# A relative-position bias table in DRAM: one copy and reversed queries in place of 128 shifted copies

## The chip, the cores and the metric

The kernel runs on one core of a Trainium2 chip. The metric is the device time of one launch in microseconds (us). A core has a matrix engine (TensorE, PE in the profile), a vector engine (VectorE, DVE), a scalar engine (ScalarE, ACT), GpSimd (POOL) and SyncE (SP), which here only issues DMAs. Each engine works through its own queue of instructions strictly in order. 16 DMA engines move the data.

## The reference

A trunk of two layers on 256 tokens of 1024 channels, all float32. Layer 0 has a feed-forward block, differential attention, a second feed-forward block and a gated embedding; layer 1 has a state-space mixer in place of the attention. What matters here is the bias of the attention scores: it depends only on the distance between query and key, through a table of 32 buckets and 16 columns (8 heads with two softmax maps each).

```
def diff_attention(h, w_qkv, w_o, lam_vecs, subln_g, rel_bias, lambda_init):
    ...
    def block(args):
        q_blk, blk = args
        q_pos = blk * Q_BLOCK + jnp.arange(Q_BLOCK, dtype=jnp.int32)
        dist = q_pos[:, None] - k_pos[None, :]
        bias = rel_bias.astype(jnp.float32)[t5_bucket(dist)]
        bias = bias.reshape(Q_BLOCK, S, N_HEADS, 2).transpose(2, 3, 0, 1)
        s = jnp.einsum('bhmqd,bhmkd->bhmqk', q_blk, k).astype(jnp.float32) + bias
        s = jnp.where(dist >= 0, s, NEG_INF)
        prob = jax.nn.softmax(s, axis=-1)
        attn = prob[:, :, 0] - lam * prob[:, :, 1]
        return jnp.einsum('bhqk,bhkv->bhqv', attn.astype(v.dtype), v)
    ...
    o = rmsnorm(o, subln_g) * (1.0 - lambda_init)
    o = o.transpose(0, 2, 1, 3).reshape(Bsz, S, D_MODEL)
    return o @ w_o
```

## The kernel before

The 256 tokens are two blocks of 128 (b = 0 and 1), each with its own x tile. Weights come as tiles of [128, 1024] float32 (512 KB, `raw`): SP issues one DMA for each, ScalarE casts it to float32r (`hi`, line 131), VectorE subtracts to get the rest (`lo`, line 133). There are three `raw` buffers, so the fourth load waits until the `lo` of the first has been computed. Both blocks use a weight tile, and every product is three matmuls: hi by hi (line 302), lo by hi (303), hi by lo (304).

The first feed-forward block works in column groups c. A group of block b has two PSUM banks (`up`), one for the gate and one for the linear part. When both are summed, ScalarE takes `sg`, the SiLU of the gate bank (line 444), VectorE multiplies it with the other bank (`h`, line 446), and TensorE transposes `h` (`hT_ps`, line 449). There are four banks in all, which the group c = 0 of both blocks fills. The first matmul of group c = 1 therefore waits for the first `sg`. Eight weight tiles make up a group.

At the start the program also prepares what the attention wants later, in low priority and so mixed into the first feed-forward block. The bias is one of these. GpSimd fills `tab` [16, 384] in 32 copies (line 535): one row for each softmax map, with the bias of distance d at index 255 - d and a large negative number from index 256 on, for keys that come after the query. Then `tab` goes to DRAM as `tab_d` [128, 16, 384], one copy per query, by eight DMAs of SP of 16 copies each (line 539): 128 x 16 x 384 x 4 bytes = 3.1 MB. In the attention a head's bias is one DMA (line 581) of 128 rows, one per query. Its partition step in DRAM is one element less than a copy, so each row starts one element earlier in its own copy. The bias tiles have three buffers; the first three loads depend on `tab_d` alone and are issued in the first feed-forward block, the other 13 in the attention. `tab` comes from the pool `work` with the tag "sg", which has two buffers and serves the `sg` tiles of the feed-forward too: the second `sg` waits until the DMAs have read `tab`.

The queries go to `qz` by a VectorE copy from PSUM (line 675, eight times), and the normalised outputs of four heads are transposed and split into `oT` by one ScalarE and one VectorE instruction (lines 321 and 322 from line 642, four times).

The order on each engine is made by a scheduler from priorities and its own estimates of time, so a change in one place can move instructions elsewhere.

Of the kernel before, what the change touches and what calls it, by code (L numbers as in the profile page):

```python
# [9 lines left out]
F32 = mybir.dt.float32  # L10
# [6 lines left out]
P = 128  # L17
# [5 lines left out]
# Places in the schedule, by layer (f01: block 0, second ffn) or by norm (block, norm, token half).  # L23
# [49 lines left out]
def bucket_ranges(n_buckets=32, max_dist=128, n=256):  # L73
    """[start, stop) of the distances in each causal T5 bucket."""
    exact = n_buckets // 2
    of = []
    for d in range(n):
        if d < exact:
            of.append(d)
        else:  # L80
            large = exact + int(math.log(d / exact) / math.log(max_dist / exact) * (n_buckets - exact))
            of.append(min(large, n_buckets - 1))
    return [(of.index(b), n - of[::-1].index(b)) for b in range(n_buckets)]


class Weights:
    """Streams weight tiles [128, 1024] from DRAM and splits each into two float32r parts, or takes two tiles unsplit."""
# [35 lines left out]
    def flush(self, force):  # L123
        """Splits what is loaded, up to the limit."""
        nc = self.nc
        while self.pending and self.pending[0][0] < max(self.split_limit, force + 1):
            n, raw = self.pending.pop(0)
            hi = self.split_pool.tile([P, 1024], F32R, tag="hi", name=f"hi{n}")
            lo = self.split_pool.tile([P, 1024], F32R, tag="lo", name=f"lo{n}")
            with self.hold[0]():  # L130
                nc.scalar.copy(hi, raw)  # L131
            with self.hold[1]():
                (nc.gpsimd if n in self.on_pool else nc.vector).tensor_tensor(lo, raw, hi.bitcast(F32), ALU.subtract)  # L133
            self.tiles[n] = (hi, lo)
# [8 lines left out]
def trunk(ctx, tc, x, p, norm_g, ffn_w_in, ffn_w_out, attn_w_qkv, attn_w_o, attn_lam, attn_subln_g,  # L143
          rel_bias, ssm_lam_re, ssm_lam_im, ssm_log_dt, ssm_b_re, ssm_b_im, ssm_c_re, ssm_c_im, ssm_d, ssm_w_glu,
          ssm_b_glu, ple_w_proj, ple_w_gate, out):
    nc = tc.nc
# [8 lines left out]
    dram = ctx.enter_context(tc.tile_pool(name="dram", bufs=1, space=bass.MemoryType.DRAM))  # L155
# [5 lines left out]
    def extra_banks(name):  # L161
        """The last two banks serve one section after another."""
        if "cm" in ps_extra:
            ps_extra["cm"].__exit__(None, None, None)
        ps_extra["cm"] = tc.tile_pool(name=name, bufs=1, space=bass.MemoryType.PSUM)
        ps_extra["pool"] = ps_extra["cm"].__enter__()
# [126 lines left out]
    def after_transposes(b, key, left):  # L293
        """The second block's last products of a layer leave room for the first block's transposes of the next."""
        at, step = OPT["at"].get(key, (0, 1))
        n = (at - left) // step + 1 if at else 0
        if b == 0 or n <= 0 or not marks.get(0):
            return nullcontext()
        return tc.issue_after(marks[0][min(2 * n, KT) - 1])
# [62 lines left out]
    def post_norm(b, halves, gain, factor, name):  # L362
        """x += factor * rmsnorm(m) with m in two [128, 512] PSUM banks."""
        xb = xs[b]
        parts = []
# [26 lines left out]
    def two_halves(b, accs, hi, lo, units, key):  # L392
        """Products over k into both halves; the last units finish the first half before the second."""
        tail = OPT["tail"].get(key, 1)
        for k in range(len(units)):
            take(b, units[k])
            ks = [k] if k < len(units) - tail else range(len(units) - tail, len(units)) if k == len(units) - 1 else []
            for j in range(2):
                sl = slice(j * 512, (j + 1) * 512)
                for kk in ks:  # L400
                    wh, wl = W.tiles[units[kk]]
                    left = (len(units) - k) * 2 if len(ks) == 1 else 2 * len(ks)
                    left -= j * len(ks) + kk - ks[0]
                    with after_transposes(b, key, left):
                        mm3(accs[j], hi[:, kk, :], lo[:, kk, :], wh[:, sl], wl[:, sl], kk == 0, kk == len(units) - 1)
            yield

# [108 lines left out]
    if any(st[0] == "attn" for st in stages):  # L516
# [7 lines left out]
        # bias of every softmax map by j = key - query + 127 (distance 255 - j), masked beyond 255  # L524
# [11 lines left out]
        # one copy per query: a stride of one less than a copy then shifts the table by the query  # L536
        tab_d = dram.tile([P, 16, 384], F32, name="tab_d")
        for j in range(8):
            nc.sync.dma_start(tab_d[16 * j:16 * j + 16].rearrange("r m j -> m r j"),
                              tab.rearrange("m (o j) -> m o j", o=1).broadcast_to([16, 16, 384]))  # L540
# [34 lines left out]
    def scores(b, h):  # L575
        kT = shared["kT"]
        nk = P * (b + 1)
        nm = f"{h}_{b}"
        bias = attn_pool.tile([P, 2, 256], F32, tag="bias", name=f"bias{nm}", bufs=3)
        src = tab_d[0, 2 * h:2 * h + 2, 127 + 256 - nk:127 + 256 - nk + 1]  # L580
        nc.sync.dma_start(bias[:, :, 0:nk], bass.AP(tensor=src.tensor, offset=src.offset,
                                                      ap=[[16 * 384 - 1, P], [384, 2], [1, nk]]))
# [34 lines left out]
    def attention(b, qkv_units, pj_units, o_units):  # L617
# [9 lines left out]
        def normed(grp, on):  # L627
# [11 lines left out]
            for h in range(4):  # L639
                nc.tensor.transpose(pt[:, h * P:(h + 1) * P], on[:, h, :], ident)  # L640
            split_T(pt, oT_hi[:, grp * 4:grp * 4 + 4, :].rearrange("p a t -> p (a t)"),
                    oT_lo[:, grp * 4:grp * 4 + 4, :].rearrange("p a t -> p (a t)"), sub_g)
# [8 lines left out]
        for n, (part, grp) in enumerate(QKV_ORDER):  # L651
# [21 lines left out]
            if part == 0:  # L673
                for m in range(2):
                    (nc.vector.tensor_copy if m >= OPT["qz"] else nc.scalar.copy)(
                        qz[b][64 * m:64 * m + 64, :, m, :], ptv[64 * m:64 * m + 64])
# [41 lines left out]
    def exact_exp(out_, in_, n, nm):  # L718
        """exp to float32 accuracy: 2^(m / 16) times a short series of the rest."""
# [14 lines left out]
    def ssm_exp():  # L734
        """lambda, lambda * dt and the moduli |a|^k with states (e, p) on partitions, columns (q, g'): group 16q + 2g' + e."""
# [20 lines left out]
    def ssm_tables(pool, keep):  # L756
# [7 lines left out]
        # sine and cosine of lambda_im * dt: reduced to [-pi, pi], polynomials of the half angle  # L764
# [24 lines left out]
        # powers of a = rho e^(i theta), then of the phase and of the modulus by squaring  # L789
# [16 lines left out]
        # phases of a^(8j), moduli of a^8  # L806
# [23 lines left out]
        # (a - 1) / lambda  # L830
# [23 lines left out]
        # the norm's gain of the input channels goes into b and d  # L854
# [11 lines left out]
        # output matrices with states on partitions  # L866
# [82 lines left out]
        # skip connection on the diagonal, Toeplitz rows to DRAM behind seven zero blocks  # L949
# [20 lines left out]
    def ssm_u(b):  # L970
        """x and the norm's factors to the layout (channel group, block) x (step, channel) through DRAM."""
# [35 lines left out]
    def ssm_core(pool, vs, tos):  # L1007
# [35 lines left out]
        def grouped(out_ap, st_, w, **flags):  # L1043
            """One product per channel group: 32 stationary columns and 128 moving columns each."""
# [288 lines left out]
```

## Time and profile before

| | |
|---|---|
| device time, median of 3 runs | 1148.12 us (1147.39 to 1149.25) |
| span of the profiled execution | 1145.0 us |
| TensorE busy | 1049.3 us (92%) |
| VectorE busy | 694.8 us (61%) |
| ScalarE busy | 554.4 us (48%) |
| GpSimd busy | 241.3 us (21%) |
| moved by DMA | 221.74 MB, mean 194 GB/s |

The span runs from the first to the last instruction of the one profiled execution. Its own device time is not listed beside it; the median of the timed runs lies 3.1 us above the span, which is what lies around it. Times inside the trace count from the span's start. "Waited for" always names what ended a wait.

### The profile page before, as it was taken

The page shows a single profiled execution, that of the slowest core. Times are in us where ns is not written, and L with a number is a line of the kernel's source. Part 1 is how long each engine was busy: PE and PEld are TensorE (multiplying, and loading weights), DVE is VectorE, ACT ScalarE, POOL GpSimd, SP SyncE. Part 2 cuts the span into 40 slices and gives each one's busy share as a digit, 9 for nine tenths or more (in the row PEclk, how much of TensorE's full clock was granted, in tenths as well). Part 3 has the DMA queues.
Part 4 walks back from the last instruction along what each step waited for, and adds up shares of the span by engine and source line. Part 5 has one row for each costly group of instructions (what it writes and reads, how often), then busy time and mean ns, then how long its engine had stood idle before and what let it go on. Part 6 is the DMA issues. An engine that isn't in the chain of part 4 may idle for free.

```text
span 1145.0 us, 14323 instructions
## 1 busy us (share of the span) xinstructions
PE 1049.3 (92%) x5123; PEld 839.2 (73%) x5123; DVE 694.8 (61%) x1011; ACT 554.4 (48%) x873; POOL 241.3 (21%) x289
## 2 busy tenths in 40 slices
PE   6599999999998999999787997999966999999997
PEld 4478888878776787777665776888744878888885
DVE  5166554659838897555678563655358576555464
ACT  5255444556765544443455542544343465444454
POOL 6000000000012004888889400000122010000001
PEclk9799999999999999999998998999987999999999
DMA  8976655646439667666556579756693557564651
GB/s 219 163 246 210 186 189 192 200 145 211 157 128 207 181 192 203 202 206 223 176 165 198 142 204 308 236 200 208 207 358 137 172 178 220 184 186 170 211 168 56
DMA packets 138103, 221.74 MB, mean 194 GB/s; under 512 B 34352, under 2 KB 63024, under 8 KB 138032
## 3 DMA queue, kind: packets, MB, share of 16 engines
q1 hardware_dynamic: 136976, 220.17, 62.8%
q8 instruction: 40, 0.66, 0.2%
q10 hardware_dynamic: 1056, 0.66, 0.2%
q14 instruction: 31, 0.25, 0.1%
HBM read 205.13 MB, written 19.86 MB: 196 GB/s over the span
## 4 chain that ended last, share of the span: by engine, by line
PE 48%; issue 19%; POOL 11%; DMA 9%; DVE 6%; ACT 4%; SPq 3%; DVEq 0%; POOLq 0%; ACTq 0%
PE up L302 7%; PE up L303 7%; PE up L304 7%; DMA raw<-in_ffn_w_in_dram 5%; PE dn L304 4%; PE dn L302 4%; PE dn L303 4%; DVE lo L133 2%; PE qkvat L302 2%; PE qkvat L303 2%; PE qkvat L304 2%; ACT hi L131 2%; POOL or L899 1%; PE sp L586 1%; DMA db<-in_ssm_d_dram 1%
## 5 line engine op out<-in xcount | busy, mean ns | idle before, releaser
L133 DVE TENSOR_TENSOR lo<-raw,hi 128x1024 fp32r<-128x1024 f32 x332 | 425.0, 1286 | 292.3 <-ACT hi L131 289.7
L131 ACT CAST hi<-raw 128x1024 fp32r<-128x1024 f32 x332 | 347.7, 1051 | 349.0 <-DMA raw<-in_ffn_w_in_dram 121.0
L302 PE MATMUL up<-hi,xThi 128*128 128x512 f32 x704 | 281.7, 403 | 22.5 <-ACT sg L444 8.9
L303 PE MATMUL up<-lo,xThi 128*128 128x512 f32 x704 | 280.3, 400 | 2.4 <-DVE lo L133 2.4
L304 PE MATMUL up<-hi,xTlo 128*128 128x512 f32 x704 | 281.6, 405 | 0.0
L302 PEld LDWEIGHTS up<-hi,xThi 128*128 128x128 f32 x704 | 135.5, 193 | 52.8 <-ACT sg L444 9.8
L303 PEld LDWEIGHTS up<-lo,xThi 128*128 128x128 f32 x704 | 135.3, 192 | 33.0 <-DVE lo L133 5.0
L304 PEld LDWEIGHTS up<-hi,xTlo 128*128 128x128 f32 x704 | 135.1, 193 | 29.2 <-issue 0.8
L302 PE MATMUL dn<-hi,hThi 128*128 128x512 f32 x352 | 138.3, 394 | 0.0
L304 PE MATMUL dn<-hi,hTlo 128*128 128x512 f32 x352 | 138.1, 393 | 0.0
L303 PE MATMUL dn<-lo,hThi 128*128 128x512 f32 x352 | 138.0, 392 | 0.0
L313 POOL TENSOR_SCALAR v_pn<-sspn,sspn 128x1 f32<-128x1 f32 x8 | 3.4, 423 | 359.9 <-ACT junkpn L370 356.9
L304 PEld LDWEIGHTS dn<-hi,hTlo 128*128 128x128 f32 x352 | 66.4, 189 | 14.1 <-issue 0.4
L303 PEld LDWEIGHTS dn<-lo,hThi 128*128 128x128 f32 x352 | 66.4, 189 | 13.9 <-DVE lo L133 0.2
L302 PEld LDWEIGHTS dn<-hi,hThi 128*128 128x128 f32 x352 | 66.4, 189 | 13.6 <-issue 0.2
L321 ACT ACTIVATE xThi<-xT_ps,gT 128x128 fp32r<-128x128 f32 x112 | 38.9, 366 | 48.7 <-PE xT_ps L339 48.4
L326 DVE TENSOR_TENSOR hTlo<-hT_ps,hThi 128x512 fp32r<-128x512 f32 (+1 forms) x48 | 30.8, 643 | 36.6 <-ACT hThi L325 36.6
L325 ACT CAST hThi<-hT_ps 128x512 fp32r<-128x512 f32 (+1 forms) x48 | 26.4, 549 | 53.2 <-PE hT_ps L449 53.1
L322 DVE SCALAR_TENSOR_TENSOR xTlo<-xT_ps,gT,xThi 128x128 fp32r<-128x128 f32 x112 | 36.5, 344 | 20.5 <-ACT xThi L321 20.2
L339 PE MATMUL xT_ps<-ident,x 128*128 128x128 f32 x112 | 31.1, 300 | 17.7 <-DVE xTlo L322 10.7
L444 ACT ACTIVATE sg<-up,r_pre 128x512 f32<-128x512 f32 (+1 forms) x48 | 30.8, 650 | 20.9 <-PE up L304 11.5
L446 DVE SCALAR_TENSOR_TENSOR h<-up,r_pre,sg 128x512 f32<-128x512 f32 (+1 forms) x48 | 33.6, 701 | 11.0 <-ACT sg L444 8.5
(352 smaller groups left out, 1296.4 us busy)
## 6 DMA issues: line engine op xcount, KB each, us to landing
raw<-in_ffn_w_in_dram SPq DMA_DIRECT2D x160, 512.0 KB, 4.4
raw<-in_ffn_w_out_dram SPq DMA_DIRECT2D x88, 512.0 KB, 3.9
raw<-in_attn_w_qkv_dram SPq DMA_DIRECT2D x24, 512.0 KB, 4.3
raw<-in_ffn_w_in_dram SPq DMA_DIRECT2D x32, 256.0 KB, 3.5
raw<-in_ple_w_gate_dram SPq DMA_DIRECT2D x16, 512.0 KB, 4.3
raw<-in_ssm_w_glu_dram SPq DMA_DIRECT2D x16, 512.0 KB, 4.2
gain<-in_norm_g_dram SPq DMA_DIRECT2D x8, 512.0 KB, 4.8
raw<-in_attn_w_o_dram SPq DMA_DIRECT2D x8, 512.0 KB, 4.0
```

The source lines that it names most:

```text
L131: nc.scalar.copy(hi, raw)
L133: (nc.gpsimd if n in self.on_pool else nc.vector).tensor_tensor(lo, raw, hi.bitcast(F32), ALU.subtract)
L302: nc.tensor.matmul(out_ap, st_hi, w_hi, start=start, stop=False)
L303: nc.tensor.matmul(out_ap, st_hi, w_lo, start=False, stop=False)
L304: nc.tensor.matmul(out_ap, st_lo, w_hi, start=False, stop=stop)
L321: return (nc.scalar.activation(hi, psum, AF.Copy, scale=scale).ins, nc.vector.scalar_tensor_tensor(lo, psum, scale, hi.bitcast(F32), ALU.m ...
L322: nc.vector.scalar_tensor_tensor(lo, psum, scale, hi.bitcast(F32), ALU.mult, ALU.subtract).ins)
L325: nc.scalar.copy(hi, psum)
L326: nc.vector.tensor_tensor(lo, psum, hi.bitcast(F32), ALU.subtract)
L339: marks[b].append(nc.tensor.transpose(pt, xb[:, k * P:(k + 1) * P], ident).ins)
L444: nc.scalar.activation(sg[:, :w], gp, AF.Silu, scale=r)
L446: nc.vector.scalar_tensor_tensor(h[:, :w], up_, r, sg[:, :w], ALU.mult, ALU.mult)
```

## The change

`tab_d` becomes one copy of the table, [16, 384] or 24.6 KB, written by one DMA that GpSimd issues. A head's bias is again one DMA of 128 rows, now with a partition step of one element: row p is the table shifted by p. That suits queries in reversed order, so the copy into `qz` reads PSUM backwards (`::-1`), and the split into `oT` reads backwards again to put the tokens back. Comments and docstrings went too, which moves line numbers by two from there on; buffer numbers in names are lower by 7 (`raw_314` is now `raw_307`).

```diff
-        # one copy per query: a stride of one less than a copy then shifts the table by the query
-        tab_d = dram.tile([P, 16, 384], F32, name="tab_d")
-        for j in range(8):
-            nc.sync.dma_start(tab_d[16 * j:16 * j + 16].rearrange("r m j -> m r j"),
-                              tab.rearrange("m (o j) -> m o j", o=1).broadcast_to([16, 16, 384]))
+
+        tab_d = dram.tile([16, 384], F32, name="tab_d")
+        nc.gpsimd.dma_start(tab_d, tab)
...
-        src = tab_d[0, 2 * h:2 * h + 2, 127 + 256 - nk:127 + 256 - nk + 1]
+        src = tab_d[2 * h:2 * h + 2, 256 - nk:256 - nk + 1]
         nc.sync.dma_start(bias[:, :, 0:nk], bass.AP(tensor=src.tensor, offset=src.offset,
-                                                      ap=[[16 * 384 - 1, P], [384, 2], [1, nk]]))
+                                                      ap=[[1, P], [384, 2], [1, nk]]))
...
-            split_T(pt, oT_hi[:, grp * 4:grp * 4 + 4, :].rearrange("p a t -> p (a t)"),
-                    oT_lo[:, grp * 4:grp * 4 + 4, :].rearrange("p a t -> p (a t)"), sub_g)
+            split_T(pt.rearrange("p (a t) -> p a t", a=4)[:, :, ::-1], oT_hi[:, grp * 4:grp * 4 + 4, :],
+                    oT_lo[:, grp * 4:grp * 4 + 4, :], sub_g)
...
                     (nc.vector.tensor_copy if m >= OPT["qz"] else nc.scalar.copy)(
-                        qz[b][64 * m:64 * m + 64, :, m, :], ptv[64 * m:64 * m + 64])
+                        qz[b][64 * m:64 * m + 64, :, m, :], ptv[64 * m:64 * m + 64, :, ::-1])
```

The order changes in the first feed-forward block only. On SP, from the fifth weight tile on, before:

```order
L119 DMA raw_308<-in_ffn_w_in_dram 128x2x512
L539 DMA tab_d<-tab 16x16x384 x3
L119 DMA raw_314<-in_ffn_w_in_dram 128x2x512
L539 DMA tab_d<-tab 16x16x384 x2
L119 DMA raw_320<-in_ffn_w_in_dram 128x2x512
L539 DMA tab_d<-tab 16x16x384 x3
L119 DMA raw_407<-in_ffn_w_in_dram 128x2x512
```

The same place with the change:

```order
L119 DMA raw_301<-in_ffn_w_in_dram 128x2x512
L119 DMA raw_307<-in_ffn_w_in_dram 128x2x512
L579 DMA bias_0_1918<-tab_d 128x2x128
L579 DMA bias_0_1936<-tab_d 128x2x128
L119 DMA raw_313<-in_ffn_w_in_dram 128x2x512
L579 DMA bias_0_1954<-tab_d 128x2x128
L119 DMA raw_400<-in_ffn_w_in_dram 128x2x512
L119 DMA raw_418<-in_ffn_w_in_dram 128x2x512
```

The eight writes are gone, and the first three bias loads have moved up by three weight tiles. The first of them waits for the landing of the one write of `tab_d`, and the weight tiles from `raw_313` on stand behind it. `raw_307` is the eighth tile, the last of group c = 0.

On GpSimd, with the change, after the copies that fill `tab`:

```order
L535 COPY tab<-rbT 16x143
L721 MEMSET exrho_224 128x32
L315 TENSOR_SCALAR v_pre_374<-ss_372 128x1
L538 DMA tab_d<-tab 16x384
L317 TENSOR_TENSOR r_pre_376<-v_pre_374,neg_half 128x1
```

Only the DMA row is new there; behind it stands the norm's factor of the second token block, which the second `sg` needs.

On ScalarE, up to the first two `sg`, before (`xThi` are parts of the normalised input, which TensorE needs for the last products of group c = 0):

```order
L321 ACTIVATE xThi_350<-xT_ps_352,gT 128x128
L131 CAST hi_316<-raw_314 128x1024
L321 ACTIVATE xThi_350<-xT_ps_353,gT 128x128
L321 ACTIVATE xThi_244<-xT_ps_247,gT 128x128
L131 CAST hi_322<-raw_320 128x1024
L444 ACT_TABLE_LOAD
L444 ACTIVATE sg_462<-up_283,r_pre_279 128x512
L444 ACTIVATE sg_540<-up_387,r_pre_383 128x512
```

The same place with the change:

```order
L131 CAST hi_309<-raw_307 128x1024
L321 ACTIVATE xThi_343<-xT_ps_345,gT 128x128
L131 CAST hi_315<-raw_313 128x1024
L321 ACTIVATE xThi_343<-xT_ps_346,gT 128x128
L321 ACTIVATE xThi_237<-xT_ps_240,gT 128x128
L131 CAST hi_402<-raw_400 128x1024
L131 CAST hi_420<-raw_418 128x1024
L131 CAST hi_438<-raw_436 128x1024
L131 CAST hi_469<-raw_467 128x1024
L444 ACT_TABLE_LOAD
L444 ACTIVATE sg_455<-up_276,r_pre_272 128x512
L444 ACTIVATE sg_533<-up_380,r_pre_376 128x512
```

The last two `xThi` have moved back behind the cast of one more weight tile (the ninth in place of the eighth), and the first `sg` behind four more (up to the 13th tile, `raw_467`).

## Rows read from the trace of the kernel before

**Rows 1.** Windows: us; busy PE, PEld, DVE, ACT, POOL; clock; DMA share; GB/s.
```profile
32.34:59.00 26.66, 13.53 (x43) 10.03 (x42) 5.18 (x8) 7.37 (x9) 0.00 (x0) 0.68 0.94 185
...
79.10:87.00 7.90, 5.67 (x21) 4.58 (x21) 5.07 (x5) 4.40 (x6) 0.00 (x0) 0.78 0.74 220
87.00:230.00 143.00, 143.00 (x650) 118.03 (x649) 81.12 (x84) 68.48 (x84) 0.86 (x2) 1.00 0.62 197
```

**Rows 2.** Waits from 20 to 95 us: total us, times, longest.
```profile
ACT hi L131 <- DMA raw<-in_ffn_w_in_dram: 33.1, 18, 10.2
...
PE up L302 <- ACT sg L444: 8.9, 2, 6.8
ACT sg L444 <- DMA tab_d<-tab: 7.8, 1, 7.8
...
PE up L302 <- ACT xThi L321: 4.2, 1, 4.2
...
PE hT_ps L449 <- DVE h L446: 2.2, 1, 2.2
```

**Rows 3.** Timeline of SP: start, us, instruction.
```profile
20.21 4.22 SPq L539 DMA_DIRECT2D tab_d<-tab  x3
...
36.88 8.28 SPq L539 DMA_DIRECT2D tab_d<-tab  x3
```

**Rows 4.** Landing of the eight writes that read `tab` (line 539).
```profile
DMA to landing us min/median/max: 5.7/10.1/13.5
```

**Rows 5.** Timeline of GpSimd: the instruction ahead of the new DMA.
```profile
20.33 1.01 POOL L315 TENSOR_SCALAR v_pre<-ss 128x1 f32<-128x1 f32 x1
```

**Rows 6.** DMA issues from 0 to 80 us: count, KB each, us to landing.
```profile
raw<-in_ffn_w_in_dram SPq DMA_DIRECT2D x22, 512.0 KB, 4.8
...
ssm_nat<-in_ssm_lam_re_dram ACTq DMA_DIRECT2D x2, 16.0 KB, 4.2
```

**Rows 7.** Landing of the 16 bias loads (line 581).
```profile
DMA to landing us min/median/max: 2.3/4.7/5.9
```

**Rows 8.** Timeline of ScalarE: start, us, instruction, idle time before.
```profile
44.97 1.28 ACT L444 ACT_TABLE_LOAD   x1
46.26 0.69 ACT L444 ACTIVATE sg<-up,r_pre 128x512 f32<-128x512 f32 x1
...
57.78 1.05 ACT L131 CAST hi<-raw 128x1024 fp32r<-128x1024 f32 x1 [0.33 <-DMA raw<-in_ffn_w_in_dram]
59.25 1.05 ACT L131 CAST hi<-raw 128x1024 fp32r<-128x1024 f32 x1 [0.42 <-DMA raw<-in_ffn_w_in_dram]
...
64.56 1.05 ACT L131 CAST hi<-raw 128x1024 fp32r<-128x1024 f32 x1 [1.35 <-DMA raw<-in_ffn_w_in_dram]
```

**Rows 9.** Timeline of TensorE: start, us, instruction, idle time before.
```profile
36.95 1.22 PE L302 MATMUL up<-hi,xThi 128*128 128x512 f32 x2 [4.21 <-ACT xThi L321]
...
44.53 0.39 PE L304 MATMUL up<-hi,xTlo 128*128 128x512 f32 x1
```

**Rows 10.** Windows, a stretch of the attention; columns as in rows 1.
```profile
255.00:285.00 30.00, 30.00 (x150) 25.40 (x149) 28.44 (x61) 19.72 (x47) 0.00 (x0) 1.00 0.69 212
```

**Rows 11.** Groups by line and form, 225 to 335 us: busy us, mean ns, idle.
```profile
L675 DVE COPY qz<-qkTat 64x512 f32<-64x512 f32 x8 | 5.5, 685 | 0.1
```

**Rows 12.** Line 326: count, ns min/median/max, first and last start, forms.
```profile
L326 DVE TENSOR_TENSOR yTlo<-y_tr,yThi x8: 414/418/426, 876.3 to 887.3; 128x256 fp32r<-128x256 f32 x8
L326 DVE TENSOR_TENSOR pTloproj<-pT_psproj,pThiproj x4: 412/414/417, 308.2 to 827.0; 128x256 fp32r<-128x256 f32 x4
```

**Rows 13.** DMA issues of the whole span, columns as in rows 6.
```profile
gain<-in_norm_g_dram SPq DMA_DIRECT2D x8, 512.0 KB, 4.8
...
bglu<-in_ssm_b_glu_dram SPq DMA_DIRECT2D x4, 256.0 KB, 7.8
```

**Rows 14.** Instructions on `bias`, 300 to 312 us: ns min/median/max, first, last start.
```profile
L589 DVE TENSOR_TENSOR s<-sp,bias x4: 672/686/693, 303.2 to 309.8; 128x512 f32<-128x512 f32 x4
L581 SPq DMA_DIRECT2D bias<-tab_d x1: 377/377/377, 304.0 to 304.0; - x1
```

## The prediction

> **What bounds the kernel now.** I read first where TensorE is not at work, since the table shows it busy for 92% of the span. From 87 to 230 us it has no gap at all and runs at the full clock (1.00, which is 2.4 GHz): 650 instructions in 143.0 us, or 0.22 us each [rows 1]. There the kernel is bound by its matmuls, and VectorE, ScalarE and the DMAs have room (81, 68 and 0.62 of the stretch). Two earlier stretches are another matter. From 32.3 to 59.0 us TensorE issues 43 instructions in 26.66 us at a mean clock of 0.68, and from 79.1 to 87.0 us 21 in 7.90 us at 0.78 [rows 1]. At 0.22 us each these would take 9.5 and 4.6 us. So the two stretches lose 17.2 + 3.3 = 20.5 us. Part of it is waiting, the rest is the time after a wait, in which the clock stands at its lower level (1.2 GHz): the 24 matmuls that end group c = 0 start from 36.95 to 44.53 us, 7.8 us with the last, after a wait of 4.21 us, where 24 x 0.22 = 5.3 would do [rows 9]. The lower clock cost 2.5 us there.
>
> Next, the waits from 20 to 95 us [rows 2]. TensorE waits for `sg` (8.9 us), `xThi` (4.2) and `h` (2.2). All three hang on ScalarE, which waits 33.1 us for weight tiles and once 7.8 us for the DMAs that read `tab`: the second `sg` needs its buffer. The queue of SP says why the tiles are late. The eight writes of `tab_d` begin at 20.2 us and the last group of them leaves SP at 45.2 [rows 3], each landing after 5.7 to 13.5 us [rows 4], and two weight tiles stand in between. In that time the DMA engines are busy for 0.94 and yet the weights don't come. So here, unlike later, the writes of `tab_d` are on the path that sets the end, and what is lost at 60 us isn't won back, since TensorE has no gap between 87 and 230 us in which to do so.
>
> **What the change removes.** The eight writes, 3.1 MB, with their place in SP's queue and their hold on `tab`. The most that this can give is all 20.5 us, if no wait takes their place.
>
> **What it puts there.** One wait does. I walk through the new order.
>
> 1. GpSimd issues the write of `tab_d` when the instruction ahead of it ends, 20.33 + 1.01 = 21.3 us [rows 5]. No DMA was issued by GpSimd before, so its landing has to be bounded. From below by the fastest bias load, 2.3 us [rows 7]; from above by the slowest old write, 13.5 us [rows 4]. I take 4.2 us, from the loads of 16 KB that ScalarE issued at 13 to 15 us [rows 6], which are nearest in size (24.6 KB) and in time. The write lands at T = 25.5 us, between 23.6 and 34.8. Behind it on GpSimd stands only the norm's factor for the second `sg`, needed much later.
>
> 2. SP waits at the first bias load until T. Before that it has issued `raw_307`, the eighth tile, whose buffer comes free in time, where the kernel before had it behind three writes. Held back are the tiles from `raw_313` on. Two bias issues at 0.38 us [rows 14] come first, so `raw_313` is issued at T + 0.8 and, with 4.8 us for a weight tile [rows 6], lands at T + 5.6.
>
> 3. The last `xThi` now stand behind the cast of `raw_313`: T + 5.6 + 1.05 = 32.2 us, and some tenths for themselves. TensorE comes to them at 36.95 - 4.21 = 32.7 us [rows 9]. This wait of 4.2 us goes, just. The 24 matmuls that end group c = 0 then take 5.3 us, to 38.1.
>
> 4. Group c = 1 needs the first `sg`, and that now stands behind the casts up to the 13th tile, `raw_467`. The steady loop of a buffer (load, cast, `lo`) is 6.8 us, 57.78 to 64.56, and neighbouring casts start 1.5 us apart, 57.78 to 59.25 [rows 8]. So the cast of `raw_436`, in the buffer of `raw_313`, starts at T + 5.6 + 6.8 = T + 12.4, that of `raw_467` at T + 13.9. With 1.05 for the cast, 1.28 for the table load and 0.69 for `sg` [rows 8] it ends at T + 16.9 = 42.4 us. TensorE has been ready since 38.1, so it waits 4.3 us and then pays the lower clock once more, 2.5 us. Left: 6.8 us.
>
> 5. The second `sg` follows at once, since `tab` was read by T. The stretch at 79 us goes too: its `sg` stands behind the eighth cast after `raw_467`, which at 6.8/3 = 2.3 us a tile comes at 42.4 - 3.0 + 18.1 = 57.5 us, and TensorE ends group c = 1 (96 matmuls) not before 42.4 + 2.5 + 96 x 0.22 = 66.0. The weights are then ahead because they flowed while TensorE waited.
>
> 6. The attention. Bias loads keep their count, rows and bytes. They land in 4.7 us now, at most 5.9 [rows 7]; the last has the tightest use, issued at 304.0 and added at 309.8, 5.8 us later [rows 14]. What is new is that all 128 rows read overlapping addresses. A row that all partitions read alike is the nearest case: `gain` lands in 4.8 us (512 KB), `bglu` in 7.8 (256 KB, four in a row) [rows 13]. I take no change; the upper end is 7.8 us.
>
> The `qz` copies and the `oT` split keep their counts and shapes and read PSUM backwards. No instruction of before does that. A permuted read is the nearest: `yTlo` takes 418 ns where the plain `pTloproj` takes 414 [rows 12], so I take nothing. The upper end is twice the time: eight copies at 0.685 us [rows 11], 5.5 us, and as much again for the eight instructions of the split. VectorE is busy for 28.44 of 30 us at 255 to 285 us [rows 10], so little of that would be covered. A gain is excluded, since no work is left out there.
>
> **The sum.** 20.5 - 4.3 - 2.5 = 13.7 us saved. It is made against the span of 1145.0 us, which becomes 1131.3; with the 3.1 us around it, unchanged, **1134.4 us**.
>
> Two rules of the Trainium skill bear on step 1. The rows give 4.2 us [rows 6]. The page DMA: Bandwidth & Descriptors, section Anatomy of one DMA, gives a DMA issued by GpSimd about 2 us plus bytes over 436 GB/s, here 2.1 us. By that estimate T is 23.4 us and the time 1132.3. Against the change speaks the page SBUF — State Buffer, section SBUF: two separate sides: a DMA issued by GpSimd can stand still while VectorE holds the port that the two share, since GpSimd can't write the descriptors; its example grows from 620 to 3100 ns. By that estimate T grows by 2.5 us and the time to 1136.9; no DMA of the trace here can show it.
>
> **The rivals.**
> - *The small write lands late.* GpSimd's first DMA, beside weight loads and a busy VectorE. For it: the old writes took up to 13.5 us. Against: theirs were 393 KB each. Every microsecond of T is one more of waiting: at T = 34.8 the sum is 13.7 - 9.3 = 4.4, so 1143.7. Nothing is left at T = 39.2. Chance 0.12. The port lock of the Trainium skill belongs here.
> - *The stretch at 79 us stays*, because the new order on ScalarE makes its `sg` late again: 3.3 us less saved, 1137.7. For it: TensorE waited for that `h` before, 2.2 us [rows 2]. Against: step 5. Chance 0.12.
> - *Weights arrive sooner than I say*, and the new wait vanishes: 20.5 us saved, 1127.6. Against: the loop of 6.8 us was measured without the writes. Chance 0.08.
> - *The weights were bound anyway, and the writes hidden:* about 1148. Against: the 7.8 us wait on `tab` and the gapless stretch after 87 us. Chance 0.03.
> - *Slower: overlapping bias rows.* If 128 rows of one place in DRAM are read one after another, a bias lands late. The 13 loads of the attention go through three buffers, so some 4.3 loads follow one another, and each microsecond beyond 5.8 costs 4.3 us. The gain is used up at 9.0 us; at 10 us the time is 1134.4 + 18.1 = 1152.5. Against: `bglu`, all rows in one place, lands in 7.8, which costs 8.6 us (1143.0). Chance 0.05.
> - *Reversed reads at twice the time*, 11 us: 1145.4. Chance 0.02.
>
> My forecast has 0.58. Its own range is 1130 to 1138, from T and the landings in steps 2 to 4. For 8 in 10 I take 1129 to 1141: that adds the rival of the stretch at 79 us, and a moderately late write. A measurement of this kernel tells about 0.2%, 2.3 us, from no change. Faster: the forecast, the first three rivals, the doubled reads, and most of a moderate delay of the bias, 0.92. Within it 0.03, slower 0.05.
>
> **What would show it.** Right: no stretch with DMAs busy and weights late at 25 to 55 us; the write of `tab_d` landing near 25.5 us and SP free then; one wait of TensorE for `sg` of some 4 us ending near 42 us, with a lower clock behind it; no other gap up to 87 us; `bias` landing below 6 us and `qz` at 0.69 us. Wrong: that write landing after 30 us, a wait for `bias` on VectorE at 255 to 310 us, longer `qz` or `oT` instructions there, or a gap near 65 us.

## The result and the profile after

| | before | after |
|---|---|---|
| device time, median | 1148.68 us (4 runs, 1147.39 to 1149.78) | 1135.51 us (4 runs, 1133.70 to 1138.04) |
| ratio | | 0.9887, 95% interval 0.9866 to 0.9908 |
| profiled execution: time, span | span 1145.0 us | 1135.24, 1133.4 us |
| written to DRAM | 19.86 MB | 16.74 MB |

The change saves 13.2 us by the medians and 11.6 by the spans of the two profiled executions; 13.7 and 1134.4 us had been predicted.

The windows of the changed kernel come first, in the stretches of [rows 1] (columns as there).

```profile
32.34:59.00 26.66, 21.86 (x92) 16.98 (x91) 16.72 (x19) 15.78 (x20) 0.00 (x0) 0.94 0.73 225
59.00:79.10 20.10, 20.10 (x94) 16.66 (x93) 10.74 (x11) 9.60 (x12) 0.00 (x0) 1.00 0.66 185
79.10:87.00 7.90, 7.90 (x36) 6.52 (x35) 4.84 (x5) 3.71 (x5) 0.00 (x0) 1.00 0.66 195
```

The reader is to see the count in the first row: 92 matmuls in the 26.66 us where there were 43, at a clock of 0.94 instead of 0.68. At 0.22 us each they need 20.2 us, so 6.4 us are still lost there. The stretch at 79 us is full. The DMA share is lower and the bytes per second are higher than before: 0.73 and 225 GB/s against 0.94 and 185.

The waits from 20 to 95 us, to be held against [rows 2]:

```profile
ACT hi L131 <- DMA raw<-in_ffn_w_in_dram: 15.3, 9, 5.5
...
PE up L302 <- ACT sg L444: 4.3, 1, 4.3
...
PE up L302 <- ACT xThi L321: 0.4, 1, 0.4
```

ScalarE waits for weight tiles half as long as before, its wait for `tab_d` is gone, and TensorE is left with one wait worth the name, the one for `sg`. Two timelines tell how the small write went. The first is GpSimd's, with the landing of the write (line 538) as the view of `tab` gives it; the second is SP's.

```profile
15.32 6.34 POOL L535 COPY tab<-rbT 16x1 f32<-16x1 f32 x32
...
21.87 1.33 POOL L315 TENSOR_SCALAR v_pre<-ss 128x1 f32<-128x1 f32 x1
23.26 0.78 POOL L538 DMA_DIRECT2D tab_d<-tab x1
...
DMA to landing us min/median/max: 2.3/2.3/2.3
```

```profile
10.40 11.36 SPq L119 DMA_DIRECT2D raw<-in_ffn_w_in_dram  x5
25.56 0.88 SPq L579 DMA_DIRECT2D bias<-tab_d  x2
26.54 0.68 SPq L119 DMA_DIRECT2D raw<-in_ffn_w_in_dram  x1
27.27 0.47 SPq L579 DMA_DIRECT2D bias<-tab_d  x1
27.85 50.35 SPq L119 DMA_DIRECT2D raw<-in_ffn_w_in_dram  x20
```

The write is issued at 23.26 and lands 2.3 us later; at 25.56 SP is free and takes the first bias load. Now what that does on ScalarE (start, us, instruction, idle time before), and the two places where TensorE waits:

```profile
31.84 1.05 ACT L131 CAST hi<-raw 128x1024 fp32r<-128x1024 f32 x1 [5.45 <-DMA raw<-in_ffn_w_in_dram]
32.80 0.62 ACT L321 ACTIVATE xThi<-xT_ps,gT 128x128 fp32r<-128x128 f32 x2
34.44 1.05 ACT L131 CAST hi<-raw 128x1024 fp32r<-128x1024 f32 x1 [1.02 <-DMA raw<-in_ffn_w_in_dram]
...
40.58 1.04 ACT L131 CAST hi<-raw 128x1024 fp32r<-128x1024 f32 x1 [1.56 <-DMA raw<-in_ffn_w_in_dram]
41.64 1.28 ACT L444 ACT_TABLE_LOAD   x1
42.93 1.27 ACT L444 ACTIVATE sg<-up,r_pre 128x512 f32<-128x512 f32 x2
```

```profile
33.21 0.77 PE L302 MATMUL up<-hi,xThi 128*128 128x512 f32 x2 [0.41 <-ACT xThi L321]
43.67 0.80 PE L302 MATMUL up<-hi,xThi 128*128 128x512 f32 x1 [4.27 <-ACT sg L444]
```

`raw_313` keeps ScalarE idle for 5.45 us. The last `xThi` come in time but for 0.41 us, and the first `sg` comes behind the cast at 40.58, so that TensorE stands for 4.27 us.

### The profile page after: what moved, and what is told of

Same layout as the page of the kernel before. It is cut to its first block, busy times and chain, and to the rows that moved or that the text cites. A ratio compares the mean times of both kernels' runs of the same rounds, so it can differ in the third digit from the quotient of the medians.

```text
span 1133.4 us, 14320 instructions
## 1 busy us (share of the span) xinstructions
PE 1048.4 (92%) x5123; PEld 836.6 (74%) x5123; DVE 693.3 (61%) x1011; ACT 553.5 (49%) x873; POOL 243.5 (21%) x290
## 3 DMA queue, kind: packets, MB, share of 16 engines
HBM read 205.13 MB, written 16.74 MB: 196 GB/s over the span
## 4 chain that ended last, share of the span: by engine, by line
PE 51%; issue 19%; POOL 11%; DMA 9%; DVE 5%; ACT 4%; SPq 1%; DVEq 0%; POOLq 0%; ACTq 0%
PE up L302 8%; PE up L303 8%; PE up L304 8%; PE dn L304 4%; PE dn L302 4%; PE dn L303 4%; DMA raw<-in_ffn_w_in_dram 4%; PE qkvat L302 2%; PE qkvat L303 2%; PE qkvat L304 2%; DMA lo<-o_d 2%; DVE lo L133 2%; PE zglu L302 1%; PE zglu L303 1%; PE zglu L304 1%
## 5 line engine op out<-in xcount | busy, mean ns | idle before, releaser
L339 PE MATMUL xT_ps<-ident,x 128*128 128x128 f32 x112 | 30.5, 295 | 17.6 <-DVE xTlo L322 10.9
L446 DVE SCALAR_TENSOR_TENSOR h<-up,r_pre,sg 128x512 f32<-128x512 f32 (+1 forms) x48 | 33.6, 701 | 11.6 <-ACT sg L444 6.9
L302 PE MATMUL qkvat<-hi,xThi 128*128 128x512 f32 x96 | 38.1, 397 | 0.2 <-ACT xThi L321 0.2
```

Of the source, the lines that this page charges most:

```text
L302: nc.tensor.matmul(out_ap, st_hi, w_hi, start=start, stop=False)
L339: marks[b].append(nc.tensor.transpose(pt, xb[:, k * P:(k + 1) * P], ident).ins)
L446: nc.vector.scalar_tensor_tensor(h[:, :w], up_, r, sg[:, :w], ALU.mult, ALU.mult)
```

## The experiments

Ratios are to the kernel before, timed beside each set of kernels on the same chip. The median of before was 1149.56 us for the first four kernels, 1149.04 for the second four, 1148.42 for the last three. The rows under an experiment are windows (columns as in [rows 1]) or timelines of the engine named in the row, as above.

### 1. The reversed reads alone

The kernel before with the new bias addresses and the two PSUM reads backwards; the eight shifted writes stay.

```diff
-        src = tab_d[0, 2 * h:2 * h + 2, 127 + 256 - nk:127 + 256 - nk + 1]
+        src = tab_d[0, 2 * h:2 * h + 2, 256 - nk:256 - nk + 1]
-                                                      ap=[[16 * 384 - 1, P], [384, 2], [1, nk]]))
+                                                      ap=[[16 * 384 + 1, P], [384, 2], [1, nk]]))
-            split_T(pt, oT_hi[:, grp * 4:grp * 4 + 4, :].rearrange("p a t -> p (a t)"),
+            split_T(pt.rearrange("p (a t) -> p a t", a=4)[:, :, ::-1], oT_hi[:, grp * 4:grp * 4 + 4, :],
-                        qz[b][64 * m:64 * m + 64, :, m, :], ptv[64 * m:64 * m + 64])
+                        qz[b][64 * m:64 * m + 64, :, m, :], ptv[64 * m:64 * m + 64, :, ::-1])
```

> The kernel before with its eight writes and 128 copies, but with reversed queries: only the direction of the PSUM reads and the sign of the partition step change. Theory (the writes are the whole cost, reversed reads are free): time within 2.5 us of the kernel before (ratio 0.998 to 1.002), `qz` copies at 0.685 us, the `oT` split at 0.67 and 0.75 us. Rival (reversed reads cost up to twice): `qz` above 1 us and up to 11 us slower, which the change would have hidden in its gain.

Measured: 1150.47 us, ratio 1.0019 (0.9997 to 1.0041). The copies into `qz`, in the view of that tile:

```profile
L675 DVE COPY qz<-qkTat x8: 672/688/695, 236.0 to 279.0; 64x512 f32<-64x512 f32 x8
```

Read backwards they take 688 ns by the median, and 685 by the mean of [rows 11] forwards. The time isn't told from that of before: by the interval it is at most 0.4% longer and not shorter by more than 0.03%, so reading backwards brings no gain that the change could owe to it. The split into `oT` takes 0.67 us on ScalarE and 0.74 to 0.75 on VectorE in both. This kernel doesn't have the single table with its overlapping rows; experiment 2 has.

### 2. The eight writes put back, with nobody waiting for them

The changed kernel, and beside its small write the eight old ones, from a copy of the table in a buffer that is not used again, to DRAM that nobody reads.

```diff
+        tab2 = attn_pool.tile([P, 6, 256], F32, tag="at", name="tab2", bufs=1) ... [0:16, 0:384]
+        nc.gpsimd.tensor_copy(tab2, tab)
+        extra_d = dram.tile([P, 16, 384], F32, name="extra_d")
+        for j in range(8):
+            nc.sync.dma_start(extra_d[16 * j:16 * j + 16].rearrange("r m j -> m r j"), ...)
```

> The changed kernel, with the eight old writes of 3.1 MB added from a second copy of the table in a buffer of its own, into DRAM that nobody reads. Theory (the writes themselves, by their place in SP's queue and on the DMA engines): the gain is gone, ratio 0.997 to 1.003, TensorE again loses about 20 us from 32 to 87 us. Rival 1 (it was the hold on the buffer of `tab` that made the second `sg` late): the gain stays for the most part, 1136 to 1140, since nothing holds that buffer here. Rival 2 (the smaller table or the reversed reading gains something by itself in the attention): half or more of the gain stays.

Measured: 1152.3 us, ratio 1.0025 (1.0008 to 1.0041). The windows:

```profile
32.34:59.00 26.66, 16.75 (x63) 11.90 (x61) 5.81 (x9) 5.60 (x8) 0.00 (x0) 0.87 0.90 135
59.00:80.00 21.00, 14.58 (x53) 11.88 (x54) 9.69 (x9) 8.81 (x11) 0.00 (x0) 0.76 0.81 224
```

The two waits of TensorE:

```profile
45.95 0.79 PE L302 MATMUL up<-hi,xThi 128*128 128x512 f32 x1 [6.66 <-ACT sg L444]
65.42 0.80 PE L302 MATMUL up<-hi,xThi 128*128 128x512 f32 x1 [7.46 <-ACT hi L131]
```

The whole loss is back although no `sg` waits for the table's buffer. It has other places: TensorE waits 6.66 us for `sg` at 45.95 us and 7.46 us for the cast of a weight tile at 65.42. So the 7.8 us for which `sg` stood for `tab_d` [rows 2] were a sign and not the cause; the writes cost by keeping the weights back. And since this kernel has the single table, its overlapping rows and the reversed reads, none of these carries the gain.

### 3. The small write issued by SP

```diff
-        nc.gpsimd.dma_start(tab_d, tab)
+        nc.sync.dma_start(tab_d, tab)
```

> The changed kernel with the one small write issued by SP in place of GpSimd. Theory: its landing stays near 25 us, so the time stays within 3 us of the changed kernel (1133 to 1138); the eighth weight tile goes out some tenths later. Rival (the gain comes from moving the write to the idle GpSimd queue): slower by 5 us or more.

Measured: 1133.19 us, ratio 0.9866 (0.9847 to 0.9885), level with the changed kernel. SP and ScalarE:

```profile
21.50 0.34 SPq L538 DMA_DIRECT2D tab_d<-tab  x1
21.93 0.38 SPq L119 DMA_DIRECT2D raw<-in_ffn_w_in_dram  x1
23.03 1.39 SPq L579 DMA_DIRECT2D bias<-tab_d  x3
```

```profile
31.70 1.05 ACT L131 CAST hi<-raw 128x1024 fp32r<-128x1024 f32 x1 [4.77 <-DMA raw<-in_ffn_w_in_dram]
...
42.97 1.27 ACT L444 ACTIVATE sg<-up,r_pre 128x512 f32<-128x512 f32 x2
```

Which queue issues the write makes no difference that can be measured. And more: the first bias load goes at T = 23.03, 2.5 us sooner than in the changed kernel, and `sg` starts at 42.97 instead of 42.93. The end of `sg` doesn't follow T as steps 2 and 4 had it. It breaks at `raw_313`: its issue by SP and its landing, in the changed kernel first, then here.

```profile
L119 SPq DMA_DIRECT2D raw<-in_ffn_w_in_dram x1: 682/682/682, 26.5 to 26.5; - x1
...
DMA to landing us min/median/max: 5.3/5.3/5.3
```

```profile
L119 SPq DMA_DIRECT2D raw<-in_ffn_w_in_dram x1: 417/417/417, 24.5 to 24.5; - x1
...
DMA to landing us min/median/max: 7.2/7.2/7.2
```

The tile goes out 2.0 us sooner and lands no sooner, where step 2 had 4.8 us for any landing. From the start of its cast to the end of `sg` the two kernels need the same, 11.8 us in the changed kernel and 12.0 here (11.3 in step 4). TensorE waits 4.88 us for `sg`.

### 4. The first `sg` ahead of the casts

The limit on how many tiles ScalarE may split is lowered until the first `sg` is issued. The casts of `raw_436` and `raw_467` come behind it.

```diff
+        if (i, f, b) == (0, 0, 0):
+            W.split_limit = up[2][0] + 3
-            nc.scalar.activation(sg[:, :w], gp, AF.Silu, scale=r)
+            act = nc.scalar.activation(sg[:, :w], gp, AF.Silu, scale=r)
+            if (i, f, b, c) == (0, 0, 0, 0):
+                W.split_limit = len(specs)
+                W.hold = (lambda: tc.issue_after(act.ins)), nullcontext
+            if (i, f, b, c) == (0, 0, 1, 0):
+                W.hold = nullcontext, nullcontext
```

> The changed kernel with the casts of the 12th and 13th weight tile ordered behind the first `sg` on ScalarE, where they stood ahead of it. Theory (step 4 of the prediction: the wait of 4.3 us for `sg` and the lower clock behind it are what is left): the wait falls below 1.5 us, the lower clock behind it goes, and the time falls by 3 to 7 us against the changed kernel, to 1128 to 1132. Rival (the weights bound this stretch anyway): TensorE waits for `lo` or `hi` of these tiles instead, and the time stays at 1134 to 1137.

Measured: 1129.84 us, ratio 0.9839 (0.9822 to 0.9856).

```profile
32.34:59.00 26.66, 26.21 (x118) 21.18 (x118) 17.85 (x20) 16.29 (x20) 0.00 (x0) 1.00 0.76 222
```

The wait for `sg` is gone and with it the lower clock: 118 matmuls instead of 92, 5.7 us of work. So what step 4 left in this stretch hangs for the most part on the place of `sg` behind the casts. By the medians the kernel is 5.7 us faster than the changed one; the span of the profiled execution is only 2.0 us shorter, and that execution (1133.17 us) was the slowest of four, the others taking 1129.56 to 1129.95. Where it lost the rest was looked for in experiments 7, 8 and 10.

### 5. Four of the writes

Experiment 2 with `range(4)`.

> The kernel after, and four of the old 393 KB writes beside its small one, from a copy of the table in a buffer that nobody waits for, to DRAM that nobody reads (eight such writes cost 16.8 us: 1152.3 against 1135.5). If each write costs its share (theory), four cost half, 8.4 us: 1142 to 1146 us, the wait of TensorE for the first sg between 4.3 and 6.7 us and a shorter wait for weights near 65 us. If the first writes fit into slack (rival: eight of them held the weights for some 32 us at about 98 GB/s and only 16.8 us were lost, so some 15 us of a delay are covered), four cost next to nothing: 1135 to 1139 us, no wait for weights near 65 us.

Measured: 1140.09 us, ratio 0.9920 (0.9894 to 0.9945). TensorE:

```profile
45.14 0.79 PE L302 MATMUL up<-hi,xThi 128*128 128x512 f32 x1 [6.78 <-ACT sg L444]
72.53 0.66 PE L449 MATMUL hT_ps<-ident,h 128*128 128x128 f32 x4 [1.74 <-DVE h L446]
```

The median lies between the two expectations. Against the changed kernel in the same set (1134.47, experiment 7) four writes cost 5.6 us; eight cost 1.0025 - 0.9873 of 1149 us by the ratios of experiments 2 and 7, 17.5. Four are a third of eight by the medians; by the intervals of the ratios half isn't excluded, but no cost at all is. That the first writes are partly covered by weights that are ahead would fit, but isn't shown. The wait for `sg` grew by 2.5 us, and there is a small one for `h`; the long wait for a weight tile near 65 us appears only with eight.

### 6. The eight writes issued by GpSimd

The kernel before, with the writes out of SP's queue.

```diff
-            nc.sync.dma_start(tab_d[16 * j:16 * j + 16].rearrange("r m j -> m r j"),
+            nc.gpsimd.dma_start(tab_d[16 * j:16 * j + 16].rearrange("r m j -> m r j"),
```

> The kernel before, its eight table writes issued by GpSimd and not by SP, so that the weight tiles no longer stand behind them in SP's queue; the first sg still waits for tab's buffer. If the writes cost through the engines' time that they take (theory), the two streams share it and little changes: 1144 to 1151 us, the stretch from 32 to 59 us again with less than 20 us of TensorE busy. If they cost through their place in SP's queue (rival), the weights come as in the changed kernel: no wait for weights between 59 and 80 us, first sg alone late: 1138 to 1143 us.

Measured: 1150.18 us, ratio 1.0018 (0.9998 to 1.0038). TensorE, and the window:

```profile
58.33 0.79 PE L302 MATMUL up<-hi,xThi 128*128 128x512 f32 x1 [20.72 <-ACT sg L444]
```

```profile
32.34:59.00 26.66, 5.94 (x26) 4.60 (x25) 3.74 (x6) 4.45 (x5) 1.06 (x1) 0.64 1.00 159
```

All waits have run together into one of 20.72 us, and the time is that of before. What stands ahead of it on ScalarE, and the landing of the weight tiles that SP issued at 24.2 and 27.1 us:

```profile
45.76 1.04 ACT L131 CAST hi<-raw 128x1024 fp32r<-128x1024 f32 x1 [14.18 <-DMA raw<-in_ffn_w_in_dram]
55.24 1.04 ACT L131 CAST hi<-raw 128x1024 fp32r<-128x1024 f32 x1 [8.43 <-DMA raw<-in_ffn_w_in_dram]
...
58.61 0.69 ACT L444 ACTIVATE sg<-up,r_pre 128x512 f32<-128x512 f32 x1 [0.33 <-DMA tab_d<-tab]
```

```profile
L119 SPq DMA_DIRECT2D raw<-in_ffn_w_in_dram x2: 368/705/1042, 24.2 to 27.1; - x2
...
DMA to landing us min/median/max: 21.5/24.8/28.1
```

The weights are issued in time and land 21.5 and 28.1 us later, where 4.8 us was usual [rows 6]. The hold on `tab` is still there, but costs `sg` only 0.33 us. The DMA engines are busy for all of the stretch and move 159 GB/s. The place in SP's queue, which the prediction named beside the writes' bytes, is not needed for the loss: the writes cost by the time of the DMA engines, from either queue.

### 7. The changed kernel again

> The changed kernel once more, for a second profile. It led the kernel before by 15.0 us at 384 us and by 11.8 us at 670 us. If the 3 us are given back because work there waits longer in the new order (theory), the second profile shows the same: a lead of 14 to 15 us at the copies of cp's stage, 10.5 to 12 us at the end of the state-space tables, span 1132 to 1135 us. If they are a matter of the granted clock, which falls in other places from execution to execution (rival), the lead at the end of the tables differs by more than 1.5 us from the first profile's, and the clock below 1.00 stands in other stretches between 480 and 700 us.

Measured: 1134.47 us (6 runs), ratio 0.9873 (0.9851 to 0.9894), span 1132.3. To see where a gain is kept, the next table has the lead over the profile of before at five places, from the start times in the views of the tiles: the first matmul with `qz` (at 253.5 us before), the first on `m_ps` (448.0), the first addition to `db` (658.4), the first `ssmA` on VectorE (836.0), the last on `gtple` (1136.4).

| lead, us | qz | m_ps | db | ssmA | last gtple |
|---|---|---|---|---|---|
| changed kernel | 14.5 | 14.0 | 12.3 | 10.9 | 11.7 |
| again (7) | 13.6 | 12.6 | 12.0 | 10.9 | 12.8 |
| small write by SP (3) | 13.6 | 12.6 | 12.4 | 11.4 | 13.6 |
| `sg` first (4) | 20.2 | 20.1 | 15.3 | 14.7 | 13.7 |
| `sg` first again (10) | 21.1 | 21.9 | 19.3 | 19.4 | 19.8 |
| `sg` first, bias late (8) | 22.2 | 21.5 | 18.1 | 17.8 | 18.9 |
| both again (11) | 22.5 | 22.0 | 22.7 | 22.8 | 22.9 |
| bias late (9) | 15.9 | 15.7 | 16.8 | 17.3 | 17.2 |
| reversed reads alone (1) | 0.6 | -1.9 | -0.5 | -1.1 | -2.2 |

Neither expectation held whole. At the end of the tables (`db`) the two profiles of one kernel agree, 12.3 and 12.0; but the second had lost only 0.6 us on the way from `m_ps`, and the first 1.7. One place where they differ is the window from 500 to 520 us, first in the first profile, then in the second:

```profile
500.00:520.00 20.00, 18.19 (x88) 13.89 (x88) 11.38 (x7) 7.39 (x10) 15.14 (x13) 0.91 0.65 206
```

```profile
500.00:520.00 20.00, 18.32 (x97) 14.22 (x96) 11.95 (x7) 9.16 (x11) 16.28 (x13) 1.00 0.71 230
```

Almost the same busy time at another clock: 9 matmuls, or 2.0 us at 0.22 each.

The last row of the table is a warning. The kernel of experiment 1 has before's order of work behind the first block, and its profile still loses 2.8 us from `qz` to the end. The profile of before is one execution too, and a fast one: with the 1.8 us that lie around the span in the other profiled executions, its 1145.0 us make some 1146.8 by estimate, where the medians of before are 1148.1 to 1149.6. Differences of 2 or 3 us along a row can belong to it.

### 8. `sg` first, and the first bias loads behind the 21st weight tile

```diff
+            if n == 20:
+                self.mark = load
-        nc.sync.dma_start(bias[:, :, 0:nk], bass.AP(...))
+        with tc.issue_after(W.mark.ins) if b == 0 and h < 3 else nullcontext():
+            nc.sync.dma_start(bias[:, :, 0:nk], bass.AP(...))
```

> The kernel with the first silu ahead of the casts (1129.84 us), and the first three bias loads moved behind the 21st weight tile, so that SP waits for the small table's write while no weight stands behind it. If the wait for that write costs nothing once sg stands first (theory: TensorE's gaps before 95 us were only 0.31 and 0.52 us), the time stays: 1128.5 to 1131 us. If the weights held for some 4 us still cost (rival), 1 to 3 us more are gained: 1126.5 to 1128.5 us. Slower than 1131 us if the bias rows are then late for their first use near 300 us.

Measured: 1126.89 us, ratio 0.9806 (0.9781 to 0.9830). That speaks for the rival, but the interval meets that of experiment 4, and the two stood in different sets. So both were run again in one, with the moved loads alone beside them.

### 9. The bias loads moved, alone

> The changed kernel with the first three bias loads behind the 21st weight tile in SP's queue, and nothing else: no weight tile waits for the table's write any more, and the first sg is still behind the casts of the first tiles on ScalarE. If the 5.5 us for which the casts wait for raw_313 are what makes sg late (theory: SP held by the write and by nothing else), they go, sg ends some 4 us sooner, TensorE's wait for it falls from 4.2 us to under 1.5 us and the lower clock behind it goes: 1128.5 to 1131.5 us. If sg's place behind 13 or 14 casts is what makes it late (rival: the casts themselves, whatever the loads do), the wait stays over 3 us: 1133 to 1136 us.

Measured: 1131.54 us, ratio 0.9853 (0.9826 to 0.9880). ScalarE and TensorE:

```profile
27.38 1.05 ACT L133 CAST hi<-raw 128x1024 fp32r<-128x1024 f32 x1 [1.59 <-DMA raw<-in_ffn_w_in_dram]
...
36.12 1.05 ACT L133 CAST hi<-raw 128x1024 fp32r<-128x1024 f32 x1 [1.06 <-DMA raw<-in_ffn_w_in_dram]
39.04 1.04 ACT L133 CAST hi<-raw 128x1024 fp32r<-128x1024 f32 x1 [1.87 <-DMA raw<-in_ffn_w_in_dram]
40.10 1.28 ACT L446 ACT_TABLE_LOAD   x1
41.39 1.26 ACT L446 ACTIVATE sg<-up,r_pre 128x512 f32<-128x512 f32 x2
```

```profile
42.13 0.73 PE L304 MATMUL up<-hi,xThi 128*128 128x512 f32 x1 [4.34 <-ACT sg L446]
```

The idle time of 5.45 us is gone: the ninth tile, `raw_313` in the changed kernel, is cast at 27.38 and not at 31.84, and no weight waits for the table's write. Yet TensorE stands for `sg` as long as before, 4.34 us, which is what the rival said. But the order of ScalarE isn't the same. The cast of the 13th tile (36.12, in the changed kernel 40.58) is 4.5 us sooner; then one cast more stands ahead of `sg` and takes 2.9 us of that back, so `sg` is 1.5 us sooner, and TensorE is ready 1.6 us sooner (37.79 in place of 39.40). Behind the 13th cast `sg` would have ended at 39.1 by these rows, an estimate, 1.4 us after TensorE was ready, as the theory had it. So this run doesn't decide between the two: the late write and the casts both set when `sg` comes. The median lies at the upper edge of the theory's range, and the interval meets that of the changed kernel.

### 10 and 11. `sg` first, and both, side by side

> The kernel with the first silu ahead of the casts once more, beside the next one on one chip. Its first median was 1129.84 us (ratio 0.9822 to 0.9856) and that of the kernel with the bias loads moved as well 1126.89 us (0.9781 to 0.983), from two calls. If the moved loads give something on top (theory), this one comes out 1.5 to 4 us above the next. If the two differ only by the chip and the execution (rival), less than 1 us lies between them.

> The first silu ahead of the casts and the first bias loads behind the 21st weight tile, once more beside the kernel with the silu alone. Theory: 1126 to 1128.5 us, TensorE without a wait between 31 and 95 us. Rival: 1128.5 to 1131 us, level with the other.

Measured: 1125.87 us (0.9795, 0.9766 to 0.9825) with `sg` first, 1124.95 us (0.9791, 0.9764 to 0.9818) with both. Both are faster than the ranges named for experiment 11. They lie 0.9 us apart, as the rival of experiment 10 said; a gain of the moved loads on top isn't shown. The kernel with both has no wait of TensorE between 31 and 95 us:

```profile
32.34:59.00 26.66, 26.66 (x123) 22.10 (x122) 16.33 (x16) 16.00 (x19) 0.00 (x0) 1.00 0.73 228
```

It has the lowest median, 2.1% below the kernel before (1.8 to 2.4). And the kernel of experiment 4 came out 4.0 us faster than the first time. Its two profiles differ behind 450 us (table above: 6.4 us of lead lost the first time, 2.1 the second), for instance here, the first profile ahead of the second:

```profile
640.00:660.00 20.00, 16.22 (x59) 12.22 (x59) 10.59 (x14) 6.70 (x8) 0.00 (x0) 0.83 0.71 184
```

```profile
640.00:660.00 20.00, 17.51 (x78) 13.68 (x77) 12.62 (x18) 9.39 (x11) 0.00 (x0) 1.00 0.72 218
```

## Why the prediction was right, step by step

**The ceiling of 20.5 us** comes out to within about 1 us. With no wait left up to 95 us, the kernel with both edits leads by 22.5 us at the first matmul with `qz`. 0.9 us of it are won before 20 us, where no edit is, and so seem to belong to the execution (9.52 us of TensorE from 10 to 20 us against 8.58), which leaves 21.6.

**Steps 1 and 2** gave T = 25.5, and 25.56 was measured, by luck: two errors cancel. The write was issued 2 us later than 21.3, since filling the table took 6.34 us and `v_pre` 1.33, and it landed in 2.3 us where I took 4.2. The page DMA: Bandwidth & Descriptors of the Trainium skill, section Anatomy of one DMA, gave 2.1 us, and the trace agrees with it (2.3). In the other eight kernels and executions with this write it took 2.1 to 4.1 us, the most in experiment 9. The port lock of the page SBUF — State Buffer, section SBUF: two separate sides, doesn't show in a landing of 2.3 us, though VectorE was busy for 1.97 us of it; whether it has a part in the 4.1 us stays open. `raw_313` was issued at T + 1.0 (T + 0.8 predicted) and its cast began 0.7 us later than predicted.

**Step 3** is right: of 4.2 us of waiting for `xThi` 0.41 are left (1.10 in the second execution, experiment 7). Group c = 0 ends at 39.4 and not at 38.1.

**Step 4** is right in its place, and in its size by some luck: the wait of 4.27 us is the 4.3 of the forecast, but `sg` ended 1.2 us later than predicted (43.6 in place of 42.4) and TensorE was ready 1.3 us later (39.4 in place of 38.1). Of the 6.4 us lost in the stretch, where 6.8 had been left, 4.8 are idle time and 1.6 the lower clock, which had been put at 2.5. In the second execution 85 matmuls start there, so 8.0 us are lost. Putting `sg` first takes the wait away (experiments 4, 10).

The count behind the cast of `raw_313` holds: 11.3 us to the end of `sg` were predicted, and 11.8 and 12.0 were measured (changed kernel, 3), 14.7 with one cast more, which takes 2.9 (9). What doesn't hold is that each microsecond of T is one of waiting. Step 2 gave every weight tile 4.8 us to land, and `raw_313` took 5.3, and 7.2 when it went out 2.0 us sooner (3), so a T that came 2.5 us sooner gained nothing. The price of the late write among the rivals hangs on the same slope; a later T wasn't tried by itself.

**Step 5** is right in its outcome: from 59 to 87 us TensorE is full. The eighth cast after `raw_467` came at 61.4 us and not at 57.5, and no wait of TensorE followed from that.

**Step 6** is right. Reversed reads cost nothing that can be measured (1). The overlapping rows show no cost either: in the changed kernel the bias loads land in 4.5 us by the median and 6.2 at most (4.7 and 5.9 in [rows 7]), and no `s` waits for one.

**The sum**: 13.7 predicted, 13.2 by the medians and 14.6 when the kernel was timed again (7). In the profiles the lead is 14.5 us at 239 us and 11.7 at the end. The prediction had taken it that nothing changes behind 87 us. Against the one profile of before, 2.8 us of lead are lost from `qz` to the end in this execution (table in experiment 7), 0.8 in another of the same kernel, 6.5 and 1.3 in two of the kernel with `sg` first. The 2.8 us are no more than the kernel of experiment 1 loses, so they don't show the assumption wrong, and the medians don't either; the 6.5 go beyond that. In the windows compared the granted clock has another level; TensorE is idle for 1.8 and 1.7 us from 500 to 520, and for 3.8 and 2.5 from 640 to 660. That the clock makes all of the difference isn't shown, and what decides after which wait it falls stays open. The time came out nearer than the span by luck (1131.3 predicted, 1133.4 measured), since 1.8 us lie around it in the changed kernel and not 3.1: that number had been taken between the span of one execution and the median of others.

**What costs in the writes** was named too broadly: their bytes, their place in SP's queue and their hold on `tab`. Only the time that they take of the DMA engines is left, since the loss comes back with no hold on `tab` (2), and from another queue with a hold that costs 0.33 us (6).

## What to carry to other kernels

A stretch where the DMA engines are busy and the bytes per second are low is worth more than the wait that is named in it: ask which transfer fills the engines, and take that out, rather than move it to another queue or free its buffer. When a stall goes, read from the order of instructions which one stands next behind the casts or loads; here that gave the remaining wait of about 4 us beforehand, and a change of order on ScalarE took it away. Two profiles of one kernel can differ by some microseconds in a later stage that nobody touched, and the profile of the kernel before is one execution too, so a difference of that size wants several profiles of both.

## What the runs showed that I had not expected

The eight writes of 1536-byte rows, all from 16 partitions, fill the DMA engines at a low rate: with them beside the weights the engines were busy for 0.90 and 1.00 of the 26.66 us and moved 135 and 159 GB/s (experiments 2 and 6), against 225 GB/s at 0.73 without them. In the kernel before, from 25 to 30 us, it was 98 GB/s at 0.89. Whether the short rows or the 16 partitions make the rate low wasn't tried. A write of 24 KB issued by SP landed in 1.5 us (experiment 3), one by GpSimd in 2.1 to 4.1. Between two runs of one kernel on different chips lay 4.0 us (1129.84 and 1125.87), more than the 1.1 us between the medians of before beside them.
